# Attention queries and keys transposed in float32, two heads at a time, and parted into high and low halves as they leave PSUM

## The chip, the cores and the metric

The kernel runs on one core of a Trainium2 chip. The metric is device time in microseconds for one execution of the whole program. The kernel before takes 2084.43 us, the median of three executions that lie between 2083.12 and 2084.66 us.

## The reference

The program is one layer of a network that works on 1024 latent tokens and 256 prompt tokens of width 1024. All arrays are float32. The change touches the queries and keys of the attention, so that is the part that matters here:

```python
    z = h @ w_in
    hq, hf_f, hf_b, hi, hg, aq, ak, av, gl = jnp.split(z, _split_points(), axis=-1)
    q = rms_norm(aq.reshape(b, l, N_HEADS, HEAD_DIM), q_norm_w)
    k = rms_norm(ak.reshape(b, l, N_KV, HEAD_DIM), k_norm_w)
    ...
        q = axial_rope(q)
        k_lat = axial_rope(k)
        k_all = jnp.concatenate([ctx_k.astype(k_lat.dtype), k_lat], axis=1)
    ...
        s = jnp.einsum('bqkgd,bskd->bkgqs', qi, kf) * scale
        p = jax.nn.softmax(s, axis=-1)
        return jnp.einsum('bkgqs,bskd->bqkgd', p, vf)
```

There are 8 query heads and 2 key/value heads of 64 channels. Latent tokens attend to 512 cached context keys and to the 1024 latent keys; prompt tokens attend to the 256 prompt keys. Ahead of this stand a normalisation modulated by a conditioning vector and the projection `w_in`; behind it follow a gated linear recurrence (the scan), the merge of both branches, an output projection and a feed-forward part.

## The kernel before

**How a product is made.** A float32 product is done on TensorE as three matmuls in the type F32R: each operand is a pair of a high part, the value rounded to F32R, and a low part, what the rounding left. The helper `split` makes the pair: ScalarE copies the value to F32R (high), VectorE subtracts that from the value (low). For the attention scores the channels of a head are only 64, so high and low parts are stacked on the 128 partitions: a query tile holds 64 rows of high parts and 64 rows of low parts, and two key tiles hold the high parts twice and the low parts twice. Two matmuls then give the whole product.

**Stages.** The front (`front_ada`, `norm1_col`, `front_z` and the loop over `steps`) normalises the tokens, transposes them to channels on partitions (`norm1_tr`, L256), and makes keys, values and the queries of heads 4 to 7 (group 1), eight column steps for each of three token tiles `t` (two of 512 latent tokens, one of 256 prompt tokens). Each step's matmuls are L563, L564 and L567. After the last step of a tile, ScalarE copies keys, values and queries out of PSUM (`kv_evac`, `q_evac`), and `front_prep` norms and rotates them (`qk_norm`, on VectorE and GpSimd). Then `z_tok(AQ, ...)` (L323 to L325) makes the queries of heads 0 to 3 (group 0); then `attention` runs, with other projections as a filler between its matmuls (`z_ch`, L306 to L308, and `z_tok`). The scan, the merge and the feed-forward part follow.

**The step that changes.** For each pair of 128-token blocks `qk_norm` leaves rotated keys or queries with tokens on the partitions. Per block, `k_stack` and `q_consume` split them into a staging tile that holds high and low parts side by side (L419 and L420 for keys, which are also written twice; L473 and L474 for queries), and put a function `late` on the list `pending`. When `late` runs, TensorE transposes the staging tile with four 128x128 transposes in F32R into a PSUM bank with the tag "t" (L425 for keys, L479 for queries), ScalarE copies the bank of 512 columns to SBUF (L428, L482), and a DMA stores it to DRAM (tensors `KS*` and `QS*`). The score matmuls later load their tiles `Kl` and `Ql` from there (`load_k`, `load_q`), each with one DMA over 128 partitions.

**What sets the order.** TensorE's order is the order in which the code is written. The other engines' and the DMA queue's order is made by a scheduler from a model of the times; `tc.high_priority` moves single instructions forward. When a `late` runs is set by a small clock in the code: `due(work)` advances a model of VectorE's time by `work` and adds 6.5; `flush(dt)` advances a model of TensorE's time and runs each pending function whose time has come. `DUE` holds the work of a key block, of a query block and the margin.

**Buffers.** PSUM has two banks with the tag "t"; the transposes of `norm1_tr` use them too. Tiles in SBUF come from rings: "G" has two buffers and holds `kT`, `qT` (the copies that wait for their store) and later `oa`; "B" has four buffers and holds `kst`, `qst` (the staging tiles), `rows`, the value tiles `Vl` and others; "E" has three buffers and holds `qa`, the rotated keys and queries, among others. All loads and stores named here are issued by one engine, SyncE (SP), in one order (`dma`, L101).

The functions that the diff touches, with their lines:

## Time and profile before

| | us |
|---|---|
| median of three executions | 2084.43 |
| the execution that was profiled | 2085.25 |
| its span, first to last instruction | 2083.5 |
| TensorE (PE) busy in it | 2026.9 |
| VectorE (DVE) busy | 1405.9 |
| ScalarE (ACT) busy | 943.1 |
| GpSimd (POOL) busy | 539.3 |

Stages on the span's own clock, read from where the named lines first and last occur: the front ends at about 112 us (L129 with the tile `rows` of 32 rows is its last transpose); `z_tok` for group 0 runs from 112 to 145 us; the last stores of `QS*` are issued at 174 us; the first score matmul (L699) starts at 177.7 us, and attention ends near 730 us. The four-transpose groups L425 and L479 occur between 76.0 and 171.5 us and nowhere else.

How to read the profile: a row of a group gives line, engine, operation, output and inputs by name, shape, the count after "x", busy time, the mean duration of one in ns, then the idle time just before with the instruction that ended it. PE is the matmul side of TensorE and PEld its weight loads; SPq is the queue of DMA issues. Matmuls overlap, so the time that one takes from the path is read from the start of it to the start of the next, not from its duration.

### The profile page before, as it was taken

What the parts mean: (1) busy time and instruction counts of PE and PEld (TensorE: products, weight loads), DVE (VectorE), ACT (ScalarE), POOL (GpSimd) and SP (SyncE); (2) the same over time, 40 slices, a digit from 0 to 9 for tenths busy, and PEclk for the clock granted to TensorE, in tenths of its full rate; (3) what the DMA queues carried; (4) which work ended last, traced back from release to release, by engine and by line L of the source; (5) the groups of instructions that cost most, each with busy time, mean ns of one, the idle gap of its engine ahead of it and who ended that gap; (6) DMA issues with size and microseconds to landing.
All of it is one profiled execution on the core that took longest, in us unless ns stands there. A gap on an engine that the chain in (4) does not pass through costs nothing.

```text
span 2083.5 us, 33949 instructions
## 1 busy us (share of the span) xinstructions
PE 2026.9 (97%) x12552; PEld 1747.1 (84%) x12552; DVE 1405.9 (67%) x2677; ACT 943.1 (45%) x1928; POOL 539.3 (26%) x577
## 2 busy tenths in 40 slices
PE   6899999999999999999999999999999999999998
PEld 5688889988899878888888888988888888888886
DVE  4784776777776788779354636776666666677786
ACT  4754555555555522222231425654555444333442
POOL 1472233432332355546112100222221210000010
PEclk9999999999999999999999999999999999999999
DMA  9464221241222255445644523764444479545773
GB/s 309 125 195 139 71 73 55 66 133 53 68 82 70 73 168 181 129 151 166 220 132 147 192 101 110 228 198 160 144 155 153 153 260 366 161 155 176 232 249 128
DMA packets 230246, 319.24 MB, mean 153 GB/s; under 512 B 18072, under 2 KB 148720, under 8 KB 230080
## 3 DMA queue, kind: packets, MB, share of 16 engines
q1 hardware_dynamic: 217664, 277.41, 41.4%
q0 software_dynamic: 12416, 39.66, 5.4%
q8 instruction: 99, 1.62, 0.3%
q14 instruction: 67, 0.55, 0.1%
HBM read 229.43 MB, written 87.57 MB: 152 GB/s over the span
## 4 chain that ended last, share of the span: by engine, by line
PE 84%; DVE 8%; DMA 3%; ACT 3%; issue 2%; POOL 1%; SPq 0%; DVEq 0%; POOLq 0%; ACTq 0%
PE ps_g L306 7%; PE ps_g L308 7%; PE ps_g L307 7%; PE ps_s L699 4%; PE ps_t L740 4%; PE ps_g L1593 2%; PE ps_g L1591 2%; PE ps_g L1592 2%; PE ps_s L1439 2%; PE ps_g L756 2%; PE ps_s L1441 2%; PE ps_s L1440 2%; PE ps_g L755 2%; PE ps_g L323 2%; PE ps_g L325 2%; PE ps_g L324 2%
## 5 line engine op out<-in xcount | busy, mean ns | idle before, releaser
L306 PE MATMUL ps_g<-hs,wsp 128*128 128x512 f32 (+1 forms) x896 | 323.5, 361 | 0.4 <-DVE adas L186 0.4
L308 PE MATMUL ps_g<-hs,wsp 128*128 128x512 f32 (+1 forms) x896 | 310.8, 347 | 0.8 <-DVE wsp L278 0.8
L307 PE MATMUL ps_g<-hs,wsp 128*128 128x512 f32 (+1 forms) x896 | 310.6, 347 | 0.0
L718 POOL TENSOR_SCALAR pexp<-pexp,rs 128x512 f32<-128x512 f32 (+1 forms) x104 | 170.6, 1647 | 363.0 <-ACT pTh L743 180.0
L277 ACT ACTIVATE wsp<-wraw 128x1024 fp32r<-128x1024 f32 x110 | 109.6, 998 | 260.5 <-PE ps_g L307 82.9
L278 DVE TENSOR_TENSOR wsp<-wraw,wsp 128x1024 fp32r<-128x1024 f32 x110 | 133.6, 1216 | 120.3 <-ACT wsp L277 120.0
L308 PEld LDWEIGHTS ps_g<-hs,wsp 128*128 128x128 f32 x896 | 170.2, 190 | 22.8 <-DVE wsp L278 1.0
L306 PEld LDWEIGHTS ps_g<-hs,wsp 128*128 128x128 f32 x896 | 170.2, 190 | 21.6 <-issue 4.8
L307 PEld LDWEIGHTS ps_g<-hs,wsp 128*128 128x128 f32 x896 | 170.7, 190 | 15.3
L743 ACT ACTIVATE pTh<-ps_t 128x512 fp32r<-128x512 f32 x200 | 118.8, 601 | 131.0 <-PE ps_t L740 126.7
L700 DVE TENSOR_REDUCE mx<-ps_s 128x1 f32<-128x512 f32 (+1 forms) x208 | 136.9, 663 | 49.6 <-PE ps_s L699 48.8
L277 ACT ACTIVATE ah<-ar 128x640 fp32r<-128x640 f32 (+1 forms) x112 | 81.0, 723 | 190.3 <-PE ps_g L1592 102.3
L710 ACT ACTIVATE pexp<-ps_s,ngm 128x512 f32<-128x512 f32 (+1 forms) x208 | 137.3, 669 | 42.4 <-DVE ngm L704 40.7
L278 DVE TENSOR_TENSOR ah<-ar,ah 128x640 fp32r<-128x640 f32 (+1 forms) x112 | 90.2, 805 | 81.1 <-ACT ah L277 80.4
L744 DVE TENSOR_TENSOR pTl<-ps_t,pTh 128x512 fp32r<-128x512 f32 x200 | 136.1, 681 | 11.9 <-ACT pTh L743 11.4
L699 PE MATMUL ps_s<-Kl,Ql 128*128 128x512 f32 (+1 forms) x416 | 127.8, 412 | 2.5 <-ACT pexp L710 2.5
L740 PE MATMUL ps_t<-ident,pexp 128*128 128x128 f32 x800 | 121.0, 273 | 2.5 <-DVE pexp L718 1.5
L323 PE MATMUL ps_g<-wsp,hs 128*128 128x256 f32 x400 | 117.1, 293 | 0.0
L325 PE MATMUL ps_g<-wsp,hs 128*128 128x256 f32 x400 | 113.4, 283 | 0.0
L324 PE MATMUL ps_g<-wsp,hs 128*128 128x256 f32 x400 | 113.0, 283 | 0.0
L756 PE MATMUL ps_g<-pTl,Vl 128*128 128x256 f32 x400 | 105.4, 286 | 4.0 <-DVE pTl L744 3.9
L755 PE MATMUL ps_g<-pTh,Vl 128*128 128x256 f32 x400 | 105.5, 284 | 1.3 <-DVE oa L765 1.0
(420 smaller groups left out, 5425.3 us busy)
## 6 DMA issues: line engine op xcount, KB each, us to landing
ar<-AF SPq DMA_DIRECT2D x112, 320.0 KB, 3.4
wraw<-in_w_ff SPq DMA_DIRECT2D x32, 1024.0 KB, 6.2
wr<-in_w_ff SPq DMA_DIRECT2D x128, 256.0 KB, 4.4
wraw<-in_w_in SPq DMA_DIRECT2D x18, 1024.0 KB, 5.9
wraw<-in_w_ada SPq DMA_DIRECT2D x16, 1024.0 KB, 5.5
AF<-a POOLq DMA_DIRECT2D x48, 256.0 KB, 2.7
AF<-t POOLq DMA_DIRECT2D x48, 256.0 KB, 2.3
wa<-in_w_ada SPq DMA_DIRECT2D x32, 256.0 KB, 5.8
```

What stands on the lines that cost most here:

```text
L277: s_.activation(hi, raw, AF.Copy)
L278: v.tensor_tensor(lo, raw, f32(hi), op=ALU.subtract)
L306: pe.matmul(out, hi[:, k, :], mh, start=(first and k == 0), stop=False)
L307: pe.matmul(out, hi[:, k, :], ml, start=False, stop=False)
L308: pe.matmul(out, lo[:, k, :], mh, start=False, stop=(last and k == kcs - 1))
L323: pe.matmul(po[:, bb, :], mh[:, off:off + P], wh[:, k % 4, :], start=(k == 0), stop=False)
L324: pe.matmul(po[:, bb, :], mh[:, off:off + P], wl[:, k % 4, :], start=False, stop=False)
L325: pe.matmul(po[:, bb, :], ml[:, off:off + P], wh[:, k % 4, :], start=False, stop=(k == KC - 1))
L699: pe.matmul(pq[:, 0:n], self.qh[:, q0:q0 + P], K[self.g][var][self.kts[i]], start=(var == 0), stop=(var == 1))
L718: NORM[(i + j) % len(NORM)].tensor_scalar(x, x, self.rs[j], None, op0=ALU.mult)
L740: pe.transpose(pt[:, a, j * P:(j + 1) * P], self.Ps[j][i][:, b * P:(b + 1) * P], ident)
L755: pe.matmul(pv[:, 0:256], V[self.g][kg][:, b, :], hi[:, a, :], start=(k == 0), stop=False)
```

## The change

The staging tiles `kst` and `qst` and their splits are gone. `late` is now put on the list once for a pair of blocks. It transposes the rotated float32 values themselves: for keys two 128x128 transposes (both key heads of a block side by side make the 128 columns), for queries four (two heads each, two blocks), in place of eight F32R transposes in either case. The bank then holds 256 columns for keys, 512 for queries, and `split` makes high and low parts as the values leave PSUM: a copy by ScalarE, a subtraction by VectorE that reads the bank too. High and low parts are stored to DRAM apart, keys once in place of twice. Each load of a `Kl` or `Ql` tile becomes two DMAs over 64 partitions. `DUE` changes from 2.2 and 2.6 per block to 3.4 and 4.4 per pair of blocks.

```diff
--- before.py
+++ after.py
@@ -32,7 +32,7 @@
 RING_OF = {
     "rows": "B", "ev": "I", "wa": "X", "xr": "X", "xn": "D", "wq": "X",
     "cosb": "X", "sinb": "X", "ck": "X", "cv": "X",
-    "kve": "I", "qe": "I", "ve": "I", "sq": "J", "sqv": "E", "qn": "D", "qa": "E", "qb": "F", "kst": "B", "qst": "B",
+    "kve": "I", "qe": "I", "ve": "I", "sq": "J", "sqv": "E", "qn": "D", "qa": "E", "qb": "F",
     "kT": "G", "qT": "G", "vst": "X", "wst": "I",
     "Kl": "X", "Vl": "B", "Ql": "F", "pexp": "X", "pTh": "D", "pTl": "E", "oa": "G", "pvt": "J",
     "ze": "I", "ident0": "K",
@@ -375,10 +375,10 @@
             run(self.gen)
 
 
-    QS = [[DR((P, 4, n), "QS%d_%d" % (g, t)) for t, (_, n, _) in enumerate(TT)] for g in range(2)]
+    QS = [[DR((2, 2, P, n), "QS%d_%d" % (g, t)) for t, (_, n, _) in enumerate(TT)] for g in range(2)]
 
     KG = [512, 512, 512, 256]
-    KS = [DR((P, 4, KG[kg]), "KS%d" % kg) for kg in range(4)]
+    KS = [DR((2, P, KG[kg]), "KS%d" % kg) for kg in range(4)]
     VS = [DR((P, KG[kg] // P, 2, P), "VS%d" % kg) for kg in range(4)]
 
     cosb = S((P, 8, 64), name="cosb")
@@ -414,19 +414,15 @@
 
     def k_stack(kr, kgv, pos):
 
-        st = S((P, 2, 2, 2, 64), F32R, name="kst")
-        kb = kr.unsqueeze(2).broadcast_to([P, 2, 2, 64])
-        s_.activation(st[:, :, 0], kb, AF.Copy)
-        v.tensor_tensor(st[:, :, 1], kb, f32(st[:, :, 0]), op=ALU.subtract)
 
         def late():
-            pt = PS("t", (P, 4, P))
-            for j in range(4):
-                pe.transpose(pt[:, j, :].bitcast(F32R), st[:, j // 2, j % 2].rearrange("p a d -> p (a d)"), ident_r)
-            e = S((P, 4, P), F32R, name="kT")
+            pt = PS("t", (P, 2, P))
+            for b in range(2):
+                pe.transpose(pt[:, b, :], kr[:, b].rearrange("p k d -> p (k d)"), ident)
+            e = S((P, 2, 256), F32R, name="kT")
             with tc.high_priority(offset=600):
-                s_.activation(e, pt, AF.Copy)
-            dma(KS[kgv][:, :, pos * P:(pos + 1) * P], e)
+                split(e[:, 0], e[:, 1], pt.rearrange("p b c -> p (b c)"))
+            dma(KS[kgv][:, :, pos * P:(pos + 2) * P].rearrange("v p n -> p v n"), e)
         pending.append((due(DUE[0]), late))
 
     def v_stack(vr, nblk, kgv, pos):
@@ -460,28 +456,24 @@
             dma(O["new_cache_k"].rearrange("(b p) d -> p b d", p=P), kn.rearrange("p b k d -> p b (k d)"))
             dma(O["new_cache_v"].rearrange("(b p) d -> p b d", p=P), ve)
         v_stack(vr, 2, kgv, pos)
-        for b in range(2):
-            k_stack(kr[:, b], kgv, pos + b)
+        k_stack(kr, kgv, pos)
 
     def q_consume(g):
         def f(pr, po):
             _, qr = qk_norm(po.rearrange("p b (h d) -> p b h d", h=4), 4, qwb, 2 * pr, pr < 4)
-            for b in range(2):
-                blk = 2 * pr + b
-                t, off = blk // 4, (blk % 4) * P
-                st = S((P, 4, 2, 64), F32R, name="qst")
-                s_.activation(st[:, :, 0], qr[:, b], AF.Copy)
-                v.tensor_tensor(st[:, :, 1], qr[:, b], f32(st[:, :, 0]), op=ALU.subtract)
-
-                def late(st=st, t=t, off=off):
-                    pt = PS("t", (P, 4, P))
-                    for h in range(4):
-                        pe.transpose(pt[:, h, :].bitcast(F32R), st[:, h].rearrange("p a d -> p (a d)"), ident_r)
-                    e = S((P, 4, P), F32R, name="qT")
-                    with tc.high_priority(offset=600):
-                        s_.activation(e, pt, AF.Copy)
-                    dma(QS[g][t][:, :, off:off + P], e)
-                pending.append((due(DUE[1]), late))
+            t, off = pr // 2, (pr % 2) * 256
+
+            def late():
+                pt = PS("t", (P, 2, 256))
+                for b in range(2):
+                    for a in range(2):
+                        pe.transpose(pt[:, a, b * P:(b + 1) * P], qr[:, b, 2 * a:2 * a + 2].rearrange("p h d -> p (h d)"), ident)
+                hi, lo = [S((P, 2, 256), F32R, name="qT") for i in range(2)]
+                with tc.high_priority(offset=600):
+                    split(hi, lo, pt)
+                for i, x in enumerate((hi, lo)):
+                    dma(QS[g][t][i, :, :, off:off + 256].rearrange("a p n -> p a n"), x)
+            pending.append((due(DUE[1]), late))
         return f
 
     pending = []
@@ -493,12 +485,12 @@
         dma(cv, I["cache_v"].rearrange("(b p) (k d) -> p b k d", p=P, k=2))
         for b in range(2):
             v_stack(cv[:, 2 * b:2 * b + 2], 2, 0, 2 * b)
-        for b in range(4):
-            k_stack(ck[:, b], 0, b)
+        for b in range(0, 4, 2):
+            k_stack(ck[:, b:b + 2], 0, b)
 
 
     clk = {"pe": 0.0, "dve": 0.0}
-    DUE = (2.2, 2.6, 6.5)
+    DUE = (3.4, 4.4, 6.5)
 
     def due(work):
         clk["dve"] = max(clk["dve"], clk["pe"]) + work
@@ -675,14 +667,17 @@
             self.pt = {}
 
         def load_q(self):
-            h, n = self.h, TT[self.t][1]
+            h, n, src = self.h, TT[self.t][1], QS[self.g][self.t]
+            a, r = h % 4 // 2, h % 2 * 64
             if n == 512:
                 x = S(dt=F32R, name="Ql")
-                dma(x, QS[self.g][self.t][:, h % 4, :])
+                for i in range(2):
+                    dma(x[64 * i:64 * i + 64, :], src[i, a, r:r + 64, :])
                 q_at[h, self.t] = x
             else:
                 x = S((P, 2, 256), F32R, name="Ql")
-                dma(x, QS[self.g][self.t][:, h % 4:h % 4 + 2, :])
+                for i in range(2):
+                    dma(x[64 * i:64 * i + 64], src[i, a].rearrange("(h d) n -> d h n", h=2))
                 q_at[h, self.t], q_at[h + 1, self.t] = x[:, 0, :], x[:, 1, :]
 
         def score(self, j, i):
@@ -773,14 +768,17 @@
     V = [[None] * 4 for _ in range(2)]
 
     def load_k(g, kg):
+
         if kg == 3:
             x = S((P, 2, 256), F32R, name="Kl")
-            dma(x, KS[3][:, 2 * g:2 * g + 2, :])
+            for i in range(2):
+                dma(x[64 * i:64 * i + 64], KS[3][:, 64 * g:64 * g + 64, :].rearrange("v p n -> p v n"))
             K[g][0][3], K[g][1][3] = x[:, 0, :], x[:, 1, :]
             return
         for var in range(2):
-            K[g][var][kg] = S((P, KG[kg]), F32R, name="Kl")
-            dma(K[g][var][kg], KS[kg][:, 2 * g + var, :])
+            x = K[g][var][kg] = S((P, KG[kg]), F32R, name="Kl")
+            for i in range(2):
+                dma(x[64 * i:64 * i + 64, :], KS[kg][var, 64 * g:64 * g + 64, :])
 
     def load_v(g, kg):
         V[g][kg] = S((P, KG[kg] // P, P), F32R, name="Vl")
```

**How instructions move.** First TensorE in a step of the front for the second token tile; `qst` and `kst` are the staging tiles, `qa` the rotated values, `xr` the normed tokens of the next column. Before:

```order
L567 MATMUL ps_g<-wsp,hs 128x512 x2
L567 MATMUL ps_s<-wsp,hs 128x512 x2
L425 MATMUL ps_t<-ident,kst 128x128 x4
L479 MATMUL ps_t<-ident,qst 128x128 x4
L256 MATMUL ps_t<-ident,xr 128x128 x2
L563 MATMUL ps_g<-wsp,hs 128x512
```

and in the changed kernel at the same place:

```order
L559 MATMUL ps_g<-wsp,hs 128x512 x2
L559 MATMUL ps_s<-wsp,hs 128x512 x2
L470 MATMUL ps_t<-ident,qa 128x128 x4
L256 MATMUL ps_t<-ident,xr 128x128 x2
L555 MATMUL ps_g<-wsp,hs 128x512
L556 MATMUL ps_g<-wsp,hs 128x512
```

Two groups of four ahead of L256 became one. Over the whole program, 12 groups stood ahead of L129 with `rows` 128x32 (the end of the front) and 22 behind it; now 7 pairs stand ahead of it (the two of cached keys, three of keys, two of queries) and 10 behind it (two of keys, eight of queries). The third key pair, which stood behind L129, now stands just ahead of it.

ScalarE, at the end of the second token tile, where it copies keys and queries out of PSUM (`kve`, `qe`); `hs` and `xnb` make the next column, which TensorE needs. Before:

```order
L436 ACTIVATE vst<-kve 128x2x64
L443 ACTIVATE kve<-ps_s 128x256
L449 ACTIVATE qe<-ps_s 128x256
L482 ACTIVATE qT<-ps_t 128x512
L473 ACTIVATE qst<-qa 128x4x64
L391 ACTIVATE sq<-kve 128x256
L436 ACTIVATE vst<-kve 128x2x64
L265 ACTIVATE hs<-ps_t,modc,s_130 128x256
L270 ACTIVATE xnb<-ps_t,modc,s_130 128x256
L436 ACTIVATE vst<-kve 128x2x64 x2
L428 ACTIVATE kT<-ps_t 128x512
L473 ACTIVATE qst<-qa 128x4x64
```

and now:

```order
L432 ACTIVATE vst<-kve 128x2x64
L439 ACTIVATE kve<-ps_s 128x256
L445 ACTIVATE qe<-ps_s 128x256
L277 ACTIVATE kT<-ps_t 128x256
L391 ACTIVATE sq<-kve 128x256
L432 ACTIVATE vst<-kve 128x2x64
L265 ACTIVATE hs<-ps_t,modc,s_130 128x256
L270 ACTIVATE xnb<-ps_t,modc,s_130 128x256
L432 ACTIVATE vst<-kve 128x2x64 x2
L391 ACTIVATE sq<-qe 128x512
L265 ACTIVATE hs<-ps_t,modc,s_130 128x256
L270 ACTIVATE xnb<-ps_t,modc,s_130 128x256
```

The copies into `qst` and half of the copies out of the transposes' banks are gone from between the columns.

SP, the queue of DMA issues, from the first stores of keys. Before:

```order
L101 DMA VS_144<-vst 128x512 x2
L101 DMA KS_139<-kT 512x1x128 x4
L101 DMA KS_140<-kT 512x1x128 x2
L101 DMA QS_0_136<-qT 512x1x128 x2
L101 DMA VS_145<-vst 128x512
L101 DMA KS_140<-kT 512x1x128
L101 DMA VS_145<-vst 128x512
L101 DMA KS_140<-kT 512x1x128
```

and now:

```order
L101 DMA VS_144<-vst 128x512
L101 DMA Vl<-VS_144 128x4x128
L101 DMA KS_139<-kT 128x2x256 x2
L101 DMA KS_140<-kT 128x2x256
L101 DMA QS_0_136<-qT 128x2x256 x2
L101 DMA KS_140<-kT 128x2x256
L101 DMA VS_145<-vst 128x512 x2
L101 DMA Vl<-VS_145 128x4x128
```

There are fewer stores of keys, and the loads of the value tiles `Vl`, whose ring "B" the staging tiles no longer fill, moved up from behind the queries' stores to between them.

## The prediction

> **What bounds the kernel now.** I read the page's totals first, then a table of windows by stage, then what TensorE (PE) waited for in the stage that changes, then the timeline of PE there.
>
> ```profile
> PE 2026.9 (97%) x12552; PEld 1747.1 (84%) x12552; DVE 1405.9 (67%) x2677; ACT 943.1 (45%) x1928; POOL 539.3 (26%) x577
> 76.00:112.00 36.00, 30.37 (x167) 23.98 (x165) 29.29 (x63) 25.53 (x62) 23.01 (x32) 1.00 0.44 135
> 112.00:145.00 33.00, 33.00 (x288) 32.96 (x289) 27.23 (x60) 19.67 (x49) 24.68 (x27) 1.00 0.58 180
> 145.00:178.00 33.00, 33.00 (x220) 28.17 (x220) 11.68 (x18) 14.37 (x30) 6.25 (x7) 1.00 0.77 236
> 178.00:730.00 552.00, 542.24 (x3933) 492.06 (x3932) 394.20 (x868) 309.70 (x729) 185.48 (x117) 1.00 0.23 74
> ```
>
> The window rows give the length, then the busy time of PE, PEld, DVE, ACT and POOL. PE is the bound over the whole program. From 112 to 178 us, the second half of the stage that changes, it never stops: what is taken off PE there is time. From 76 to 112 it is idle for 36.00 - 30.37 = 5.6 us, with DVE and ACT busy for 29 and 26 of 36 us: there ACT and DVE set part of the pace. The idle time goes to four waits (us in total, times, longest):
>
> ```profile
> PE ps_t L256 <- ACT xnb L270: 2.3, 3, 1.2
> PE ps_s L567 <- DVE hs L271: 1.7, 1, 1.7
> PE ps_t L256 <- ACT kT L428: 1.2, 3, 0.4
> PE ps_t L425 <- ACT qT L482: 0.5, 1, 0.5
> ```
>
> Three of them are waits for a bank "t" that ACT has yet to empty.
>
> **The change part by part.** First the transposes on PE. How long a group holds PE is the distance from its start to the next start (start, duration, instruction):
>
> ```profile
> 84.85 0.46 PE L425 MATMUL ps_t<-ident,kst 128*128 128x128 f32 x4
> 85.14 0.41 PE L256 MATMUL ps_t<-ident,xr 128*128 128x128 f32 x2
> 85.31 0.48 PE L563 MATMUL ps_g<-wsp,hs 128*128 128x512 f32 x1
> ...
> 66.59 0.60 PE L256 MATMUL ps_t<-ident,xr 128*128 128x128 f32 x4
> 66.94 0.47 PE L563 MATMUL ps_g<-wraw,hs 128*128 128x512 f32 x1
> ...
> 115.26 0.28 PE L325 MATMUL ps_g<-wsp,hs 128*128 128x256 f32 x1
> 115.38 0.45 PE L425 MATMUL ps_t<-ident,kst 128*128 128x128 f32 x4
> 115.67 0.35 PE L323 MATMUL ps_g<-wsp,hs 128*128 128x256 f32 x1
> 115.86 0.28 PE L324 MATMUL ps_g<-wsp,hs 128*128 128x256 f32 x1
> ```
>
> Four F32R transposes take 0.29 us (84.85 to 85.14, 115.38 to 115.67). L256 is a float32 transpose against the same identity, which is what the changed kernel uses: four take 0.35 us, two 0.17. The first matmul behind a group costs 0.07 us extra (0.19 to the next start against 0.12 in the same loop).
>
> ```profile
> L425 PE MATMUL ps_t<-ident,kst x56: 223/244/279, 76.2 to 138.2; 128*128 128x128 f32 x56
> L479 PE MATMUL ps_t<-ident,qst x80: 222/243/253, 88.4 to 171.5; 128*128 128x128 f32 x80
> ```
>
> That is 136 transposes, 34 groups. In the front 12 groups, 12 x 0.29 = 3.5 us, become five of two and two of four, 5 x 0.17 + 2 x 0.35 = 1.6 us: **-2.0 us** (their neighbour is L256 both times, so the extra 0.07 stays). Behind the front 22 groups, 22 x (0.29 + 0.07) = 7.9 us, become two of two and eight of four, 2 x 0.24 + 8 x 0.42 = 3.8 us: **-4.1 us**, in the stretch where PE never idles.
>
> [...]
>
> Then ACT and DVE. Removed are the splits into staging tiles and ACT's copies of 512 columns; ACT gets a copy of 256 or 512 columns, DVE a subtraction of as many, out of PSUM:
>
> ```profile
> L482 ACT ACTIVATE qT<-ps_t 128x512 fp32r<-128x512 f32 x20 | 12.1, 606 | 18.6 <-PE ps_t L479 8.7 <-DMA QS<-qT 4.9 <-DMA KS<-kT 2.7
> L428 ACT ACTIVATE kT<-ps_t 128x512 fp32r<-128x512 f32 x14 | 8.5, 611 | 11.6 <-PE ps_t L425 9.2 <-issue 1.5 <-DMA QS<-qT 1.0
> L473 ACT ACTIVATE qst<-qa 128x256 fp32r<-128x256 f32 x16 | 6.8, 422 | 1.6 <-POOL qa L412 1.6
> L474 DVE TENSOR_TENSOR qst<-qa,qst 128x256 fp32r<-128x256 f32 x16 | 8.6, 538 | 3.7 <-ACT qst L473 3.7
> L449 ACT ACTIVATE qe<-ps_g 128x256 f32<-128x256 f32 x14 | 4.9, 390 | 0.8 <-PE ps_g L325 0.8
> L744 DVE TENSOR_TENSOR pTl<-ps_t,pTh 128x512 fp32r<-128x512 f32 x200 | 136.1, 681 | 11.9 <-ACT pTh L743 11.4
> ```
>
> ACT loses 34 x (0.42 + 0.61) = 35 us and gains 7 x 0.39 + 10 x 0.61 = 9 us. DVE loses 34 x 0.54 = 18 us and gains 10 x 0.68 + 7 x about 0.4 (an estimate between half of L744 and L474) = 10 us. Behind 112 us this is hidden by PE. In the front it bears on the four waits. L256 waited for kT (1.2 us) where a step held two or more transpose groups and the two banks ran out; now each step holds at most one pair ahead of L256, so I take **-1.2 us**. The waits for xnb and qT (2.3 + 0.5 us) come after the burst of copies out of PSUM, where ACT now has one copy less ahead of the column and two `qst` copies less: I take half, **-1.4 us** (bounds 0 and -2.8). The wait for hs (1.7 us) hangs on DVE, whose work shrinks little: 0 (bounds -1.7 and +1).
>
> What is added: a bank "t" is now free only when DVE has subtracted, and a query pair needs both buffers of ring "G", each of which must have been stored. Rows on that (us to landing are the last column of the issue rows):
>
> ```profile
> ACT qT L482 <- DMA QS<-qT: 4.9, 1, 4.9
> ACT qT L482 <- DMA KS<-kT: 2.7, 1, 2.7
> ACT kT L428 <- DMA QS<-qT: 1.0, 1, 1.0
> QS<-qT SPq DMA_DIRECT2D x20, 256.0 KB, 3.1
> KS<-kT SPq DMA_DIRECT2D x14, 256.0 KB, 2.6
> Ql<-QS SPq DMA_DIRECT2D x20, 256.0 KB, 3.2
> L101 SPq DMA_DIRECT2D Ql<-QS x20: 319/320/1123, 148.3 to 708.0; - x20
> ```
>
> ACT already waits for landed stores at times, 8.6 us in all, and none of PE's four waits names a store. Now DVE can wait too, and queued behind its subtraction are `hs` (the low part of a column, which PE needs within three steps) and the norms. In the front the seven pairs stand one step (about 3 us) or more apart. I take 0.3 us for each, **+2.0 us**; the bounds are 0 and one landing, 2.6 to 3.1 us, at each of the hand-overs, below. PE also waits directly for rotated values now, without the split between. The tightest is the fourth query pair of group 1:
>
> ```profile
> 120.17 1.29 POOL L412 TENSOR_TENSOR qa<-qa,qb 128x512 f32<-128x512 f32 x1
> 111.88 0.24 PE L129 MATMUL ps_t<-ident,rows 32*128 32x32 f32 x1
> ```
>
> Its rotation ended 121.46 - 111.88 = 9.6 us after L129; in the new order 93 matmuls of 0.12 us and two pairs stand between, 11.8 us, so 2 us are left: 0.
>
> DMAs: seven stores fewer, 34 loads more, each some 0.3 to 0.5 us of SP's time over 600 us, when SP mostly waits for others: 0. Group 1's first `Ql` loads took 3.2 us to land and were issued from 148.3 us on, 29 us ahead of the first score; cover enough for two halves: 0. In attention the same matmuls stand in a shifted mix, since the shorter `due` clock leaves about 8 us of filler (96 matmuls of 512 columns and 48 of 256 ahead of the first score become 75 and 24) for later. PE idled 552.00 - 542.24 = 9.8 us there: 0, bounds -2 and +3. Behind attention PE's order is the same.
>
> **The sum:** -2.0 - 4.1 - 1.2 - 1.4 + 2.0 = -6.7 us on the profiled span of 2083.5, so 2076.8. That execution took 2085.25 us with what lies around the span, 0.8 above the median; taken off the median, 2084.43 - 6.7 = **2077.7 us**.
>
> **The rivals.** (a) *The front swallows its share.* If DVE's chain of norms sets the pace from 76 to 112 us (its 29.3 of 36 us speak for it, PE's waits for ACT banks against), only the 4.1 us behind the front remain, less some 0.5 of new waits: 2080.8. (b) *The whole idle time goes.* ACT's relief clears all four waits and none comes new: -6.1 - 5.6 = -11.7, 2072.7. The wait for hs, which is DVE's, speaks against. (c) *Slower: ring "G" locks the front.* Key and query pairs there alternate; at four hand-overs a copy or a subtraction waits until the store before has landed (3.1 us and 0.5 of issue), and the next column's parts stand behind it: 4 x 3.6 = 14.4 in place of my 2.0, so -6.7 + 12.4 = +5.7, 2090.1. It decides from (6.7 + 2.0) / 4 = 2.2 us per hand-over. For it speak the three waits for stores above; against it that pairs are a step apart and that PE never waited through them. [...] (e) *The change moves the attention's mix for the worse*, three to seven us of new bubbles among 552, so that it comes out as no change, about 2083. The 9.8 us of idle time there show that bubbles exist; that ACT and DVE are busy for only 56% and 71% speaks against.
>
> **How the numbers follow.** Chances: my sum 0.54, (a) 0.17, (b) 0.11, (c) 0.08, (d) 0.02, (e) 0.08. The predicted time is that of the sum. Around it the bounds above give about 2075 to 2080.5; the range reaches (b) and most of (e): 2073 to 2083, which leaves out about 0.2. A measurement of this kernel can tell 0.2%, 4.2 us, from no change; so faster means below 2080.3. The sum is nearly all below (0.50), (b) all (0.11), (a) somewhat less than half (0.08), (e) little (0.02): 0.71. Within 0.2%: 0.19. Slower: (c), (d) and a rest of (e), 0.10.
>
> **What would show it.** [...] I am wrong if PE waits on POOL or DVE ahead of the transposes of queries, or if the front's length does not shrink by at least 3 us.

## The result, and the profile after

| | time, us | runs | ratio to before, 95% interval |
|---|---|---|---|
| before | 2084.55 | 6 (2080.06 to 2086.99) | |
| changed | 2071.54 | 6 (2067.11 to 2075.55) | 0.9936 (0.9922 to 0.9951) |
| changed, measured again | 2072.36 | 5 (2069.79 to 2073.08) | 0.9940 (0.9927 to 0.9954) |

The forecast was 6.7 us less, 2077.7 us with a range from 2073. The kernel became 12 to 13 us faster: the sign was right, but the forecast held only about half of the gain, and the measured time lies below its range. Left out of the medians and ratios of this document are two executions far above all others of their kernels, one of 4068 us of the changed kernel with the copies put back and one of 7127 us of the kernel before.

The profiled execution after took 2072.85 us, span 2071.1. Its totals and windows by stage (the same events stand a few us earlier now: 76 to 106 us is the second half of the front, up to 138 the query projection of group 0, up to 160 the filler ahead of the first score):

```profile
PE 2018.6 (97%) x12470; PEld 1738.5 (84%) x12470; DVE 1402.8 (68%) x2660; ACT 921.9 (45%) x1877; POOL 541.5 (26%) x577
76.00:106.00 30.00, 27.99 (x140) 22.22 (x138) 23.58 (x51) 17.65 (x43) 19.35 (x26) 1.00 0.43 139
106.00:138.00 32.00, 31.83 (x263) 31.55 (x264) 27.20 (x55) 13.73 (x33) 25.08 (x29) 1.00 0.60 184
138.00:160.00 22.00, 21.97 (x116) 18.54 (x115) 13.58 (x18) 7.06 (x12) 9.49 (x10) 1.00 0.63 201
160.00:725.00 565.00, 552.91 (x4011) 500.72 (x4010) 395.30 (x869) 310.27 (x731) 187.03 (x118) 1.00 0.23 76
```

PE idles 30.00 - 27.99 = 2.0 us in the front, where it was 5.6. ACT is busy for 59% of that window, before for 71%. In attention PE idles 565.00 - 552.91 = 12.1 us, a little more than the 9.8 of before. PE's waits from 76 to 138 us:

```profile
PE ps_t L256 <- DVE kT L278: 1.2, 2, 0.8
PE ps_t L256 <- ACT xnb L270: 0.8, 1, 0.8
PE ps_t L421 <- DVE qa L412: 0.2, 1, 0.2
```

The waits for `hs` (1.7 us) and for `qT` (0.5) are gone, that for `xnb` fell from 2.3 to 0.8, and the bank of `kT` is waited for as long as before (1.2 us), now for VectorE. The transposes themselves, on the timeline of PE (start, duration, instruction):

```profile
105.75 0.24 PE L129 MATMUL ps_t<-ident,rows 32*128 32x32 f32 x1
...
109.61 0.60 PE L470 MATMUL ps_t<-ident,qa 128*128 128x128 f32 x4
109.97 0.36 PE L323 MATMUL ps_g<-wsp,hs 128*128 128x256 f32 x1
110.17 0.28 PE L324 MATMUL ps_g<-wsp,hs 128*128 128x256 f32 x1
```

Four float32 transposes hold PE for 0.36 us, as the forecast took from L256 (0.35). The row above is a landmark: the last transpose of `rows`, the end of the front's busy part, stood at 111.88 and now stands at 105.75. Distances between the starts of such common instructions give where the span went:

| stretch | before, us | after, us | difference |
|---|---|---|---|
| start to the last transpose of rows | 111.9 | 105.7 | -6.1 |
| to the end of the query projection of group 0 | 33.3 | 31.6 | -1.7 |
| filler and attention, to their last matmul | 590.1 | 591.8 | +1.7 |
| seam, to the first scores of the scan | 9.2 | 5.6 | -3.6 |
| scan, to its last output transpose | 282.7 | 280.4 | -2.3 |
| rest of the program | 1047.8 | 1047.6 | -0.2 |

Half of the gain lies in the front. The surprise is the seam between attention and the scan together with the scan, 5.9 us, where the change removes nothing. A second profiled execution of each kernel gives -6.0 us in the front, -1.7 in the projection, -5.0 in seam and scan, but -0.4 in filler and attention and -1.1 in the rest: a single row is good to about 2 us. At the seam PE waits for the masked keys of the scan's first unit (`usf`), which VectorE makes. Before, PE's first transpose of the scan and VectorE's queue:

```profile
739.60 0.55 PE L938 MATMUL ps_t<-ident,usf 128*128 128x128 f32 x3 [3.02 <-DVE usf L909]
733.71 1.21 DVE L876 TENSOR_TENSOR_SCAN ucp<-R,uf 128x512 f32<-128x512 f32 x1
734.84 1.19 DVE L877 TENSOR_TENSOR_SCAN usf<-uf,R 128x511 f32<-128x511 f32 x1
735.96 1.21 DVE L278 TENSOR_TENSOR wsp<-wraw,wsp 128x1024 fp32r<-128x1024 f32 x1
...
738.23 1.31 DVE L909 TENSOR_TENSOR usf<-usf,um 128x512 f32<-128x512 f32 x1
```

and after:

```profile
731.23 0.44 PE L936 MATMUL ps_t<-ident,usf 128*128 128x128 f32 x2 [0.79 <-DVE usf L907]
728.01 1.21 DVE L874 TENSOR_TENSOR_SCAN ucp<-R,uf 128x512 f32<-128x512 f32 x1
729.14 1.19 DVE L875 TENSOR_TENSOR_SCAN usf<-uf,R 128x511 f32<-128x511 f32 x1
...
730.49 0.68 DVE L907 TENSOR_TENSOR usf<-usf,um 128x512 f32<-128x512 f32 x1
733.50 1.21 DVE L278 TENSOR_TENSOR wsp<-wraw,wsp 128x1024 fp32r<-128x1024 f32 x1
```

Before, the split of a weight (L278) stood ahead of `usf` on VectorE; after, it stands behind. PE's stall fell from 3.02 to 0.79 us. In the windows around the longer stall, and behind one of 2.2 us at 893 us, the granted clock was low too. The windows below give PE's busy time and, last but two, the clock; the first three rows are before, the last two after:

```profile
725.00:735.00 10.00, 7.43 (x44) 0.83 0.35 118
735.00:745.00 10.00, 6.98 (x71) 0.83 0.70 224
895.00:905.00 10.00, 10.00 (x74) 0.86 0.61 193
```

```profile
725.00:735.00 10.00, 8.62 (x84) 1.00 0.28 83
735.00:745.00 10.00, 10.00 (x79) 1.00 1.10 355
```

The low clock is not simply what the stall made. In finer windows it is 0.50 from 730.6 to 734.0 us, ahead of the stall, and again from 740.8 to 744.2 and from 894.4 to 897.8 us. In the second trace of the kernel before, the same stall took 2.94 us and the clock from 740 to 750 us was 1.00; there the seam took 7.6 us in place of 9.2. Of the 5.9 us, 2.2 are the shorter stall and about 3.4 the last two low stretches, each of which cost PE 1.7 us by the clock (3.41 us at 0.50).

### The profile page after: what moved, and what is told of

It reads as the page before. It is cut to its first block, busy times and chain, and to the rows that moved or that the text cites. A ratio compares the mean times of both kernels' runs of the same rounds, so it can differ in the third digit from the quotient of the medians.

```text
span 2071.1 us, 33713 instructions
## 1 busy us (share of the span) xinstructions
PE 2018.6 (97%) x12470; PEld 1738.5 (84%) x12470; DVE 1402.8 (68%) x2660; ACT 921.9 (45%) x1877; POOL 541.5 (26%) x577
## 4 chain that ended last, share of the span: by engine, by line
PE 82%; DVE 7%; DMA 3%; ACT 2%; issue 2%; POOL 1%; SPq 0%; DVEq 0%; POOLq 0%; ACTq 0%
PE ps_g L306 7%; PE ps_g L308 7%; PE ps_g L307 7%; PE ps_s L694 4%; PE ps_t L735 3%; PE ps_g L1589 2%; PE ps_g L1591 2%; PE ps_g L1590 2%; DMA wraw<-in_w_in 2%; PE ps_s L1437 2%; PE ps_s L1439 2%; PE ps_s L1438 2%; PE ps_g L751 2%; PE ps_s L1589 2%; PE ps_s L1590 2%; PE ps_s L1591 2%
## 5 line engine op out<-in xcount | busy, mean ns | idle before, releaser
L278 DVE TENSOR_TENSOR wsp<-wraw,wsp 128x1024 fp32r<-128x1024 f32 x110 | 134.6, 1225 | 122.4 <-ACT wsp L277 120.5
L307 PEld LDWEIGHTS ps_g<-hs,wsp 128*128 128x128 f32 x896 | 170.0, 190 | 15.1
L278 DVE TENSOR_TENSOR ah<-ar,ah 128x640 fp32r<-128x640 f32 (+1 forms) x112 | 89.8, 801 | 83.0 <-ACT ah L277 82.7
L751 PE MATMUL ps_g<-pTl,Vl 128*128 128x256 f32 x400 | 105.7, 287 | 7.5 <-DVE pTl L739 7.4
```

What stands on the lines that cost most here:

```text
L278: v.tensor_tensor(lo, raw, f32(hi), op=ALU.subtract)
L307: pe.matmul(out, hi[:, k, :], ml, start=False, stop=False)
L751: pe.matmul(pv[:, 0:256], V[self.g][kg][:, b, :], lo[:, a, :], start=False, stop=(k == last))
```

## Experiments

The table gathers all runs by the same landmarks: idle time of PE between 76 us and the last transpose of rows; the query projection; filler and attention together, with PE's idle time from the first score on; and the seam. The times are medians, the other columns come from one profiled execution of each.

| kernel | time, us | front idle | projection | filler + attention | attention idle | seam |
|---|---|---|---|---|---|---|
| before, again | 2084.4 | 5.6 | 33.3 | 590.2 | 9.9 | 7.6 |
| before, seam filled | 2082.5 | 4.3 | 33.3 | 591.1 | 10.6 | 8.1 |
| before, product on VectorE | 2081.8 | 5.6 | 33.3 | 590.2 | 10.2 | 6.3 |
| before, shorter due clock | 2093.6 | 9.2 | 35.9 | 595.2 | 12.6 | 5.7 |
| before, both mends | 2080.6 | 4.5 | 33.3 | 590.4 | 9.8 | 6.1 |
| queries only | 2086.3 | 4.9 | 33.2 | 596.5 | 15.1 | 9.3 |
| queries only, keys early | 2081.8 | 4.8 | 33.1 | 586.5 | 9.3 | 9.3 |
| keys only | 2089.2 | 3.7 | 37.1 | 594.4 | 13.6 | 9.2 |
| keys only, keys early | 2084.2 | 3.6 | 38.0 | 589.3 | 10.8 | 9.4 |
| changed, again | 2072.4 | 2.0 | 31.6 | 589.8 | 12.2 | 5.7 |
| changed, transposes twice | 2080.7 | 1.4 | 34.3 | 590.6 | 12.0 | 5.6 |
| changed, staging work back | 2078.4 | 3.0 | 37.4 | 589.3 | 12.3 | 5.6 |
| changed, copies back | 2073.9 | 3.3 | 31.2 | 589.8 | 12.3 | 5.7 |
| changed, old due clock | 2084.2 | 1.6 | 30.6 | 597.2 | 16.1 | 10.6 |
| changed, 8 us more filler | 2081.3 | 2.0 | 31.6 | 593.3 | 13.6 | 9.4 |
| the same, keys early | 2074.3 | 2.0 | 31.6 | 586.7 | 8.9 | 9.4 |
| changed, both mends | 2071.8 | 2.0 | 31.6 | 585.8 | 9.1 | 8.3 |
| changed, product on VectorE | 2072.4 | 2.0 | 31.6 | 588.8 | 11.9 | 7.1 |

**Both kernels again.** No edit.

> The kernel before, once more and unchanged, so that its granted clock is listed run by run. Theory (the clock carries a part of the gain): its runs lie between 2080 and 2087 us, the mean clock is 0.994 to 0.996, and the slower runs are those with the lower clock, about 4 us for 0.002. Rival (the clock has nothing to do with it): the times spread by the same 7 us with no order in the clocks.

> The changed kernel, once more and unchanged, as the base for the other runs. Theory: 2067 to 2076 us, median near 2071.5, ratio 0.9936 within 0.0015, mean clock 0.996 to 0.998. Rival (the first measurement was a lucky draw, the true gain is the forecast's 6.7 us): median 2077 to 2078.

Measured: 2084.44 us (11 runs, 2082.48 to 2087.38) with a clock of 0.994 to 0.996, and 2072.36 us with 0.997 to 0.998. In the first six runs of the changed kernel the three of 0.997 and 0.998 took 2067.1 to 2070.2 us and the three of 0.996 took 2072.9 to 2075.6. The gain is no lucky draw. The clock seems to be a part of it: the means, 0.9949 and 0.997, differ by 0.002, which on PE's 2020 us is some 4 us. The order is not strict, though: in the second measurement of the changed kernel the execution with the highest clock, 0.998, was the slowest of five (2073.1 us). In the two traces the stretches below full clock cost PE 7.7 us before and 4.5 us after (busy time times one minus the clock, over all windows of 5 us).

**The seam, from two sides.** First PE's idle time there, and at the later stall of 2.2 us, is filled with transposes of the identity ahead of the real ones, which overwrite them (the argument is their number); then the cause of the stall on VectorE is moved:

```diff
-        units[0].keys_t()
+        units[0].keys_t(32)
...
-                units[i + 1].keys_t()
+                units[i + 1].keys_t(24 if i == 12 else 0)
```

> The kernel before with idle TensorE time in the scan filled: 32 transposes of the identity (2.8 us) ahead of the scan's first transpose, where TensorE waited 3.0 us, and 24 (2.1 us) ahead of the transpose that waited 2.2 us at 891 us. They are overwritten by the real transposes, so nothing that is computed changes. Theory (the clock drops because of these two stalls): the stretches at 730, 740 and 893 us with a granted clock of 0.66 to 0.72, which lost 1.5 + 1.7 + 1.6 = 4.8 us, are gone or fewer, and the time falls by 3 to 5 us, to about 2080. Rival (the drops come by chance, or from the poorer stretch ahead of the seam): the clock drops as often, and the time stays at 2084.5 or rises by up to 0.5 us for transposes that outlast the stall.

```diff
-            g_.tensor_tensor(e[:, 0:n], k[:, 0:n], e[:, 0:n], op=ALU.mult)
+            (v if (h, d, t) == (0, 0, 0) else g_).tensor_tensor(e[:, 0:n], k[:, 0:n], e[:, 0:n], op=ALU.mult)
```

> The kernel before with one product of the scan's first unit (e = k x e, 128x512) moved from GpSimd to VectorE, so that the masked keys (usf) which TensorE waits for at the seam stand on VectorE ahead of the next unit's second scan and of a weight split, not behind them. Nothing ahead of 715 us changes. Theory (the stall of 3.0 us at the seam comes from the place of usf in VectorE's queue, and the low clock behind it from the stall): the stall falls under 1 us, the stretches of low clock at 730 to 745 us go, and the time falls by 3 to 5 us, to 2080 to 2081.5. Rival (the stall is the length of the chain of scans itself, and the clock drops by chance): it stays at 2 us or more, time within 1 us of 2084.5.

> The same move of one product in the changed kernel, where the stall at the seam is only 0.8 us because the weight split already stands behind usf. Theory (the seam fell well by the shift of filler, and can be made well in both kernels): the stall goes, the time falls by 0.5 to 1 us, and the distance between the two kernels shrinks from 12.5 us to 8 to 9 us, which is what the front and the projections gained. Rival (the seam has no part in the gain): both kernels move alike, and the distance stays at 12 to 13 us.

Measured: 2082.48 us, ratio to before 0.9994 (0.9985 to 1.0003); 2081.80 us, 0.9992 (0.9984 to 1.0001); and in the changed kernel 2072.36 us, 0.9946 (0.9934 to 0.9958). Beside the kernel before (2084.12 and 2083.73 us, measured with them) the first two are 1.6 and 1.9 us less by the medians, under the 3 to 5 expected, and both intervals still hold no change. With the seam filled, the low stretches behind 740 and 893 us are gone in the trace, while the one ahead of the seam stays (0.83 from 725 to 735 us). In the changed kernel the move is worth nothing: the wait for `usf` gives way to one of 2.2 us for `oa`, as below. The distance between the two kernels with the product moved is 9.4 us by the medians, between what theory (8 to 9) and rival (12 to 13) expected. With the product on VectorE, in the kernel before, PE's waits from 725 to 745 us and the window there:

```profile
PE ps_g L756 <- DVE pTl L744: 1.9, 2, 1.8
PE ps_g L306 <- DVE oa L765: 1.5, 1, 1.5
PE ps_g L755 <- DVE ze L851: 0.3, 1, 0.3
...
725.00:745.00 20.00, 16.38 (x147) 13.92 (x146) 19.73 (x37) 5.06 (x10) 12.96 (x12) 0.91 0.47 148
```

The wait for `usf` is gone: it did come from its place in VectorE's queue. Another took its place, for a bank "g" that VectorE's last `oa` has yet to leave, and the clock is still only 0.91. So the seam is a queue on VectorE with more than one late item, and mending the first gives only part of the 3.6 us.

**The parts of the change.** Queries alone and keys alone, each with the other half as before (the due clock of the changed half new, of the other old).

> Only the queries are changed (QS in halves, one late group per pair); the keys are staged and copied as before. 20 of the 34 old groups go. Theory (the front gained because ACT and DVE were relieved of staging and copies): the last transpose of rows (111.9 us before, 105.8 us with the whole change) comes near 108.5, since the two query pairs of the front carry 4 of 12 groups and half of the staged columns; time 2074 to 2079 us. Rival (it is the number of groups per step that counts, and the keys' groups are the ones that crowd the front): the last transpose of rows stays above 110.5.

> Only the keys are changed (KS in halves, one late group per pair); the queries are staged and copied as before. Theory (relief of ACT and DVE): the last transpose of rows comes near 109, 3 us earlier than before; time 2077 to 2082 us. Rival (groups per step): it comes at 107 or earlier, since the keys carry 8 of the front's 12 old groups, and the queries alone give little.

Measured: 2086.26 us, ratio 1.0004 (0.9993 to 1.0015), and 2089.23 us, 1.0024 (1.0014 to 1.0034). Both expectations of the time failed: neither half gains, and keys alone lose 4 to 5 us. The front's gains do add up: its idle time fell by 0.8 and 2.0 us, and the last transpose of rows, less the idle time ahead of 76 us, came 1.4 and 4.3 us earlier against 6.2 with both (each against the mean of the two traces of the kernel before). Its place, 111.3 us with queries only, is what the rival expected, and 108.6 with keys only what the theory did, so these two runs do not tell relief from the number of groups. With queries only, one of the new waits did come on top: PE stood 2.9 us at 93 to 96 us for a bank that VectorE had yet to empty into `qT`. What was gained in the front was lost behind it. With queries only, PE's waits from 425 to 445 us with the window behind them, and SP's issues (their minimum, median and maximum in ns, then start, duration, instruction):

```profile
PE ps_s L699 <- DMA Kl<-KS: 5.5, 1, 5.5
...
440.00:445.00 5.00, 5.00 (x23) 4.00 (x23) 1.00 (x7) 2.98 (x8) 0.00 (x0) 0.75 0.00 0
```

```profile
L101 SPq DMA_DIRECT2D Kl<-KS x14: 338/428/3617, 110.9 to 709.8; - x14
...
425.81 0.39 SPq L101 DMA_DIRECT2D wraw<-in_w_ada  x1
426.31 1.57 SPq L101 DMA_DIRECT2D wraw<-in_w_in  x1
427.94 4.09 SPq L101 DMA_DIRECT2D Kl<-KS  x2
```

The last block of keys for the second group of heads is loaded behind two weight loads of 1 MB each. Two issues of `Kl` take 4.1 us there, where the median of one is 0.43, and PE stands for 5.5 us; behind that the clock is 0.75. In the kernel before, the last two loads stand behind the same weights too, but they are issued 3 and 6 us after them and take 0.42 and 0.43 us; with keys only two issues stand right behind them again and take 4.4 us. In these kernels it is being right behind them that goes with the long issue. In the changed kernel the same queue has the keys first:

```profile
413.44 2.50 SPq L101 DMA_DIRECT2D Kl<-KS  x4
416.35 0.39 SPq L101 DMA_DIRECT2D wraw<-in_w_ada  x1
418.62 0.38 SPq L101 DMA_DIRECT2D wraw<-in_w_in  x1
```

**The keys loaded earlier**, in both halves:

```diff
-  for kg, a in enumerate((8.95, 8.85, 7.9))]
+  for kg, a in enumerate((10.2, 10.1, 10.0))]
```

> The run with only the queries changed, and in it the loads of keys are issued 10.2 to 10.0 steps ahead of their unit in place of 8.95 to 7.9, so that the third block of keys stands ahead of the two weight loads (1 MB each) in SP's queue. Theory (the half lost what the front had gained to the wait of 5.5 us for those keys at 430 us and to the low clock behind it): that wait goes, idle time in attention falls from 15.1 to about 10 us, and the time falls by 5 to 8 us, to 2079 to 2081. Rival (the half is slow because of the filler's mix at large): the idle time turns up elsewhere and the time stays within 2 us of 2086.3.

> The same move of the loads in the run with only the keys changed. Theory: the wait of 5.4 us at 430 us and the stretch of low clock behind it (3.1 us lost) go, the time falls by 5 to 9 us, to 2081 to 2084; the stall of 3.2 us ahead of the first late query transposes at 111 us stays. Rival: within 2 us of 2089.2.

Measured: 2081.78 us, 0.9983 (0.9974 to 0.9992), and 2084.23 us, 1.0003 (0.9993 to 1.0012): 4.5 and 5.0 us less than without, where the theory expected 5 to 8 and 5 to 9. The wait for keys is gone from both traces, and attention's idle time falls from 15.1 to 9.3 and from 13.6 to 10.8 us. The rival, that the mix at large makes the halves slow, falls for this part. The other loss of keys only stays: 4 to 5 us in the projection, with 3 to 4 us of idle time at the first late transposes of staged queries.

**The due clock and the filler.** Four kernels move nothing but the place of late groups and filler, the last also that of the keys' loads: the shorter clock in the kernel before, the old one in the changed kernel, and 8 us more filler ahead of attention in the changed kernel, without and with the keys loaded early.

```diff
-    DUE = (2.2, 2.6, 6.5)
+    DUE = (1.7, 2.2, 6.5)
```

```diff
-    DUE = (3.4, 4.4, 6.5)
+    DUE = (4.4, 5.2, 6.5)
```

```diff
         flush(1.0)
+    fz.add(8.0)
     attention(fz)
```

> The kernel before with nothing but a shorter due clock: 1.7 and 2.2 for a block of keys and of queries in place of 2.2 and 2.6, which makes 3.4 and 4.4 for two, as in the change. No instruction is added or removed, so PE's busy time stays. Theory (a part of the gain comes from filler that is left for later, so that the seam between attention and the scan falls better): the first score comes some 6 to 8 us earlier, the stall at the seam falls from 3.0 us to about 1, fewer stretches of low clock, and the time falls by 2 to 5 us, to 2080 to 2082. Rival (the mix of filler is neutral): 2084.1 within 1 us, with the stall at the seam as before. The front can move by up to 1 us either way.

> The changed kernel with the old due clock, 4.4 and 5.2 us for a pair in place of 3.4 and 4.4; no instruction is added or removed, and the loads of keys still stand ahead of the weight loads. Theory (front, projections and TensorE's saving make 8 to 9 us, and the rest hangs on where the filler falls): front and query projection within 0.5 us of the change, the rest between -1 and +5 us by the stalls at 430 us and at the seam, so 2071 to 2077. Rival (the shorter due clock is what made the gain): the front's idle time is back at 4 us or more and the time at 2080 or more.

> The changed kernel with 8 us more of filler run ahead of attention, so that the first score stands about as far behind the query projection as in the kernel before. Theory (the idle time in attention grew because 8 us of filler moved into it): idle TensorE time between the first score and the end of attention falls back from 12 us to about 10 us, and the time falls by 2 to 4 us, to 2068. Rival (the idle time there comes and goes with any shift of the mix, and more filler ahead means less cover at the end): time within 1.5 us of the changed kernel, the idle time at other places; or longer by 1 to 3 us if the end of attention runs out of filler.

> The changed kernel with 8 us more filler ahead of attention (2081.3 us) and the same move of the loads. Theory: of the 9 us that the added filler cost, the wait of 3.9 us for keys at 425 us and the low clock behind it (2.2 us) go, 4 to 6 us, so 2075.5 to 2077; the stall at the seam (3.5 us) stays, for the weight split still stands ahead of usf on VectorE. Rival: within 2 us of 2081.3.

Measured: 2093.56 us, ratio 1.0042 (1.0027 to 1.0057); 2084.17 us, 1.0000 (0.9991 to 1.0008); 2081.26 us, 0.9984 (0.9975 to 0.9993); 2074.34 us, 0.9958 (0.9945 to 0.9972). The expectations for the first three failed. In the kernel before, the seam did fall well (0.8 us of stall), but the staging was now too late for the clock; PE's longest waits between 100 and 165 us there, and with the old clock in the changed kernel between 76 and 735 us:

```profile
PE ps_t L479 <- DVE qst L474: 6.7, 2, 4.6
```

```profile
PE ps_s L694 <- ACT pexp L705: 7.1, 5, 3.7
PE ps_g L751 <- DVE pTl L739: 5.5, 9, 1.3
```

So the short clock needs the change: without the splits a query pair is ready early. And the change needs the short clock, though not for the front, which with the old one is even better (1.6 us idle; the rival had the time right and its reason wrong). With it the pending loop runs filler for 38 us ahead of the first score in place of 22; attention then has that much less, its idle time rises to 16.1 us, the seam falls badly (10.6 us) and the whole gain is lost. That the lack of filler makes attention idle is not shown by this: with 31 us of filler ahead and the keys early it idles 8.9 us. Eight microseconds of filler alone cost 9; with the keys loaded early 7 of these come back, more than the 4 to 6 expected. The theory there, that too little filler ahead makes attention idle, was wrong in sign as it stood and held only once the wait for keys (3.9 us) was away.

**What was removed, put back in the changed kernel.** PE's time (each new transpose twice), the staging's work, and ACT's copies, the last two as tiles that nobody reads. The diff shows one place of each; the other half of the transposes, the keys' staging and two copies of 256 columns for a key pair go likewise:

```diff
-                pe.transpose(pt[:, b, :], kr[:, b].rearrange("p k d -> p (k d)"), ident)
+                for i in range(2):
+                  pe.transpose(pt[:, b, :], kr[:, b].rearrange("p k d -> p (k d)"), ident)
...
+                st = S((P, 4, 2, 64), F32R, name="qst")
+                s_.activation(st[:, :, 0], qr[:, b], AF.Copy)
+                v.tensor_tensor(st[:, :, 1], qr[:, b], f32(st[:, :, 0]), op=ALU.subtract)
...
                     split(hi, lo, pt)
+                    s_.activation(S((P, 2, 256), F32R, name="qst"), pt, AF.Copy)
```

> The changed kernel with each of the 54 new transposes issued twice into the same place: 54 x 0.087 = 4.7 us of TensorE's time is given back, 1.6 us of it in the front and 3.1 us behind it; nothing else changes. Theory (TensorE's time counts in full where it never idles, and in the front about in full too): the time rises by 4 to 5 us, to about 2076.5. Rival (the change's gain comes from ACT's and DVE's relief and the clock, and TensorE's own saving is hidden): it rises by under 2 us.

> The changed kernel with the removed staging put back as work that nobody reads: for every block of keys and of queries ACT's copy (0.42 us) and VectorE's subtraction (0.54 us) into a ring-B tile. TensorE's instructions and their order are as in the changed kernel. Theory (the front's idle time went because ACT and VectorE lost the staging): TensorE's idle time between 76 us and the last transpose of rows rises from 2.0 to 3.5 us or more, and the front gets longer by 1.5 to 3 us. Rival (it went because there are fewer groups and each holds a bank for less time in the queue): the idle time stays at 2.5 us or less.

> The changed kernel with ACT's removed copies out of PSUM put back as work that nobody reads: behind each split of a key pair two more copies of 256 columns (0.39 us each), behind each query pair one more of 512 (0.61 us), so that ACT's copies take as long as before and a bank is held longer. TensorE's order is unchanged. Theory (it is the copies in ACT's queue, ahead of the column copies, that made the front idle): idle time between 76 us and the last transpose of rows rises from 2.0 to 3 us or more. Rival (the staging or the number of groups made it): it stays at 2.5 us or less. Behind the front nothing is expected to move in either.

Measured: 2080.74 us, ratio 0.9977 (0.9969 to 0.9986); 2078.40 us, 0.9972 (0.9961 to 0.9983); 2073.87 us (five executions), 0.9954 (0.9942 to 0.9967). PE's 4.7 us count in full and more than expected: 8.4 us by the medians, and by the ratios 0.37%, 7.7 us; the two profiled executions, both with a clock of 0.998, are 5.0 us apart (2078.07 and 2073.08 us). The traces give a growth of 4.2 to 4.4 us between the last transpose of rows and the first score; where the rest lies was not settled. The work put back on ACT and VectorE raises the front's idle time from 2.0 to 3.0 us (staging), between what theory and rival expected, and to 3.3 us (copies), which the theory of ScalarE's copies did expect (3 us or more). In the trace with the copies back PE waits again for ACT, from 76 to 110 us:

```profile
PE ps_t L256 <- ACT xnb L270: 2.2, 2, 1.8
PE ps_t L256 <- ACT kst L427: 1.1, 1, 1.1
```

With the staging back, the larger loss is behind the front, where the rotation is late for the first query pair (PE's waits from 76 to 150 us):

```profile
PE ps_t L480 <- POOL qa L412: 3.5, 1, 3.5
```

Neither brought back the wait for `hs`.

**Both mends in both kernels.** The keys loaded early and the product on VectorE, in the changed kernel also the 8 us of filler.

> The kernel before with the keys' loads issued early and the one product of the scan moved to VectorE. Theory (the two places behind the front are worth 2 to 4 us to the kernel before, and the rest of the distance is the change's own): 2080 to 2082 us. Rival (the mends do for the kernel before what the change did, so that the change itself is worth little): 2076 us or less.

> The changed kernel with 8 us more filler ahead of attention, as the kernel before has it, with the keys' loads early and the product of the scan on VectorE. Theory: the stall at the seam (3.2 us in the run without the product moved, 2074.3 us) falls under 2 us and its low clock goes, 2071 to 2073 us, and the distance to the kernel before with the same mends is 8 to 10 us. It would beat the changed kernel only below 2069. Rival (the gain of 12.5 us is bound to the filler's place in the changed kernel): 2075 or more.

Measured: 2080.55 us, ratio 0.9986 (0.9975 to 0.9996), and 2071.79 us, 0.9933 (0.9918 to 0.9948). The distance is 8.8 us by the medians and 0.53%, 11 us, by the ratios: what the change is worth with both places mended in both kernels. The rest of the 12 to 13 us, some 1 to 4 us, went with where the filler happened to fall. The seam still stumbles in both, so the second expectation held in its time and not in its reason: with `usf` out of the way PE waits 1.8 us for `pTl` and then for `oa`, 1.3 us before and 2.2 us in the changed kernel, and each trace has one low stretch there (0.66 from 730 to 735 us before, 0.74 in the same window in the changed kernel). The mended version is not told apart from the changed kernel (2071.5 and 2072.4 us), so no version here beats the changed kernel.

## Why the prediction was right in sign and short in size

- **PE's transposes, -2.0 and -4.1 us.** The durations were right (0.36 us for four, against 0.35; the front's term comes out of its own working as 1.9), and putting 4.7 us of PE's time back cost all of it and more. In the trace the projection of group 0 is 1.7 us shorter, and filler plus attention, where the two mended kernels can be compared, 590.4 - 585.8 = 4.6 us. Of these, 1.7 us are a stretch of half clock that falls into attention's end in the one trace and into the seam in the other, and 0.7 us are idle time; with the projection 3.9 us are left, against 4.1 forecast. No run shows a ground for rival (d), which has 0.02 in the chances: a float32 transpose held PE for 0.09 us (0.36 for four), an F32R one for 0.07 (0.29 for four), so the 54 new ones make 4.9 us where the 136 old ones made 9.9.
- **The front's waits.** This is one term that failed in size. The sum had -1.2 (`kT`), -1.4 (`xnb`, `qT`), 0 (`hs`) and +2.0 for new waits, of which the front carries most: close to nothing. Measured was an idle time 3.6 us lower. The `xnb` and `qT` waits fell by 2.0 us (forecast 1.4). The `kT` wait stayed at 1.2 us with VectorE as its releaser, so the new waits did come, but in the place of the old one and not on top (with queries only, 2.9 us did come on top). And the `hs` wait, taken as 0 because VectorE's work hardly shrinks, went altogether. It is absent or shorter (0.7 us) in every kernel whose late groups fall on other steps, the one with only a shorter due clock included, and did not come back with the work of VectorE or ACT; so by these runs it hung on the order of the steps and not on the load. Putting staging and copies back returned 1.0 and 1.3 us; if the two add up, the rest of the 3.6 us is about this wait.
- **Attention's mix, "0, bounds -2 and +3".** This, with the next point, is the step that failed most. In the first two traces, projection, filler and attention together gained nothing (-1.7 + 1.7 us), where the sum had -4.1, and seam and scan gained 5.9, where it had nothing. Moving filler is not neutral here: with no instruction added, the time moved by 9 to 12 us (shorter due clock before, old due clock and 8 us of filler in the changed kernel). The two mechanisms that could be shown are the place of the keys' loads right behind the 1 MB weight loads on SP (5 us, with low clock behind; a risk of the halves and of more filler, which neither the kernel before nor the changed one met) and the place of `usf` in VectorE's queue at the seam. The forecast did look at SP ("0") and at `Ql`, but not at `Kl` at 430 us.
- **"Behind attention PE's order is the same"** was true and not enough: VectorE's order was not, and the seam and the scan gave 5.9 us. In the profile before, the stall of 3.0 us on `usf` and the low clock (0.66 from 730 to 735 us) were there to be read; the forecast did not price them.
- **The rivals.** (b), the whole idle time of the front goes and the sum is -11.7, was nearest in its number, 2072.7, but not in its reason: 2.0 us of idle time stayed. (a) and (c) are out: the front shrank by 6.1 us and no wait of PE in it leads back to a store. (e) is half right: the mix did worsen by some 2 us of idle time, and could have by more.
- **What was to show it.** First score 18.4 us earlier (the forecast's 6.7 us and its 8 us of moved filler make 14.7), idle time in attention 12.1 us (9.8 with bounds -2 and +3), PE busy 8.3 us less (the two terms of the transposes make 6.1; part of the 8.3 is clock), a wait of L256 for a copy of `kT` (taken away with -1.2 in the sum; it stayed, for VectorE).

Between the two mended traces the parts fit: the front 5.0, the projection 1.7, filler and attention 4.6 and the scan 0.5, less 2.2 at the seam, is 9.6 us, against 9 to 11 measured. Behind the scan, where the kernels are alike, that trace of the changed kernel lost 3.4 us, about half of them to a stretch of half clock at 1385 us. What stays open is why giving back 4.7 us of PE's time cost some 8 us by the medians, and how the new order of the steps took the wait for `hs` away.

## What to carry to other kernels

Where one engine is 97% busy and filler is placed by a clock of estimates, a small edit shifts what stands behind what on the other queues, and that shift can be worth as much as the edit (here 9 to 12 us for the worse, against the 9 to 11 that the edit is worth). Before pricing an edit, look in the profile for the one-off stalls (a load behind large loads on SP, a product behind a split on VectorE at a stage's end) and for the low clock around them, and make them robust in both kernels, so that the edit is measured and not its luck. And do not test a change in halves without looking at the stalls: both halves looked worthless here, though their front gains added up.

## What the runs showed of the hardware

**A stall can cost more than its length, through the clock, and where it falls in time decides.** In these traces the granted clock is 1.00 or 0.50, and its changes lie on a grid of 3.41 us: in the kernel before, the low stretches of 3.41 us start at 730.56, 740.80 and 894.40 us, 3 and 45 such steps apart; in the changed kernel at 59.23 and 492.72 us, 127 steps apart. Each pair of rows below is one step and the step behind it, with its length, PE's busy time and, last but two, the clock. The first pair is the kernel before, the second its second trace, the third the changed kernel:

```profile
891.01:894.42 3.41, 1.43 (x9) 1.29 (x10) 3.41 (x6) 0.60 (x1) 3.41 (x5) 1.00 0.46 172
894.42:897.84 3.42, 3.42 (x9) 2.24 (x7) 3.38 (x7) 0.00 (x0) 0.43 (x1) 0.50 0.00 0
```

```profile
739.32:742.73 3.41, 1.82 (x10) 1.60 (x11) 3.35 (x9) 0.60 (x1) 2.63 (x4) 1.00 0.92 291
742.73:746.15 3.42, 3.42 (x44) 2.54 (x43) 3.38 (x3) 0.00 (x0) 3.42 (x3) 1.00 1.09 351
```

```profile
878.41:881.82 3.41, 1.69 (x8) 1.06 (x6) 3.41 (x5) 0.00 (x0) 3.33 (x4) 1.00 0.96 308
881.82:885.23 3.41, 2.92 (x15) 2.53 (x16) 3.41 (x7) 0.60 (x1) 2.35 (x3) 1.00 0.03 11
```

The first and the third pair hold the same stall of 2.2 us, the second the one of 2.9 us. Only where PE was busy for 1.43 us of the step, and not for 1.69 or 1.82, did half clock follow. Over the 20 traces, from 130 to 2055 us, all 29 steps with PE busy for at most 42% were followed by a step at half clock, of the 47 steps with 43 to 56% only 14 were, and of those above it a single one, which stood at half clock itself. In the three traces of the rows above, steps begin at 740.80, 739.32 and 738.48 us: the grid stands elsewhere in each, and the like stalls of 2.2 us fared differently. A low step in which PE is always busy costs it 1.7 us by the clock, half of its length. From start to start, a matmul of 512 columns took 0.43 us in the low step from 894.4 us and 0.23 at 889 us, at full clock, by which the step cost 1.6 us. PE was not idle throughout the step ahead of a low one: it worked for 1.25 us in the one ahead of 730.56 us and for 1.43 us in the first row.

**An issue of a DMA can take over 3 us of SP's time.** Right behind two loads of 1 MB, two loads of 256 KB took 4.09 us to issue (427.94 us, above), one of them 3.6, against a median of 0.43 us for one in that kernel. The next load on SP was issued at 432.13 us, behind them. Why an issue takes so long no run here shows.
